# The first norm's factor moved behind its products, x turned unscaled, and the last columns ended in two pieces

## The chip, the cores and the metric

The kernel runs on one core of a Trainium2 chip. The metric is the device time of one execution in microseconds (us). Engines are named as the profile names them: PE (TensorE), DVE (VectorE), ACT (ScalarE), POOL (GpSimd), SP (SyncE, which here only issues DMAs).

## The reference

Two transformer blocks follow each other on x of 256 tokens and 1024 channels. The change touches the first norm with the product behind it, and the last norm:

```python
def _rms_norm(x, g):
    y = xf * lax.rsqrt(jnp.mean(xf * xf, axis=-1, keepdims=True) + EPS)
    return y * g
...
h = _rms_norm(x, g_pre_mix[l])
proj = h @ w_in[l]
qa, ka, va, c_q, c_kv, k_r, gate_logits = _split_cols(proj, [512, 512, 512, 384, 256, 32, 2048])
...
gates = sigmoid(gate_logits + b_gate[l])
...
return rms_norm(x, final_norm_g)
```

Rope then turns qa, ka and k_r by the positions; c_q and c_kv go through norms of their own into further products; two causal attentions of 8 heads use them; gates weigh their outputs. A second block with another attention and a routed table of 16384 experts follows, and its last product with the table `expert_v` ends in the last norm.

## The kernel before

Tokens lie on the 128 partitions in two halves, `tb` 0 and 1. Each product in float32 precision is made of three products of halved numbers (`mm3`, line 173): every operand is held as a rounded part (`hh`, `wh`) and a rest (`hl`, `wl`). A weight piece arrives by a DMA of SP into `raw`, ACT rounds it into `wh` (line 124), and DVE or POOL subtracts for `wl` (line 130). The pieces take turns: of three, two rests go to DVE and one to POOL.

The first norm (`norm_parts`, line 237, called at line 457) works on a half of x in this order: ACT squares x in two pieces with a sum (line 215), DVE makes the factor 1/sqrt in ten small instructions (`rsqrt`, lines 199 to 208), DVE multiplies x by factor and gain into `ny` (line 243), PE turns `ny` in eight 128x128 squares into two PSUM tiles `tps` (line 154), ACT copies each as `hh` (line 182) and DVE subtracts for `hl` (line 183). The gain row `g_pre_mix` is a DMA that ACT issues and that writes 512 KB, one copy of the row for each partition. The second half's turn is deferred (`defer`, `tick`) until the first half's products with the first weight block are issued.

`project` (line 273) then makes the columns of `w_in` block by block: 384 columns (c_q), 288 (c_kv and k_r), and three times 512 (qa, ka, va); each block has 24 products for each half of the tokens. What is done with a result stands in `emit_cq`, `emit_ckv`, `emit_rot` and `emit_va` (lines 480 to 496): ACT copies the sum from PSUM into `cnat`, and rope or a norm follows. The angles of rope are made by DVE (lines 538 to 547) and ACT (lines 548 to 550, with a load of ACT's table ahead) from the constants `cst` and the positions `post`. The columns of the gates come turned the other way, tokens along the free dimension (`stations`, line 314), in eight units between the heads of the attentions; `gate_done` lets ACT apply tanh to each.

At the end `v_units` adds up the products with `expert_v` in four PSUM tiles `po[tb][b]` of 512 columns. The last two units are ordered so that the tokens of half 0 end first, then columns 0 to 511 of half 1, then columns 512 to 1023 of it. `finish` (line 1131) follows each: DVE adds the residual (line 1136), ACT squares (line 1137), POOL multiplies by the gain (line 1138); after a half's second piece DVE makes the factor, ACT scales 512 columns (line 1142) and DVE the other 512 (line 1144), and ACT and SP each issue a DMA of the output.

All instructions are recorded by a framework that simulates a timeline to set the order on each engine; PE's matmuls are held in the written order (`in_line`). On an engine instructions run in the order that was set. Each of the DMA issues of SP and ACT takes one of eight semaphores in turn and waits until the transfer eight issues earlier has landed.

Of the kernel before, what the change touches and what calls it, by code (L numbers as in the profile page):

```python
# [9 lines left out]
F32 = mybir.dt.float32  # L10
# [23 lines left out]
RBUFS = 4  # L34
GAP = 120

# [43 lines left out]
def block_kernel(ctx: ExitStack, tc: tile.TileContext, a, out, dbg=None):  # L80
# [61 lines left out]

    def matmul(p, x, y, start, stop):
        in_line(pe.matmul(p, x, y, start=start, stop=stop))  # L144

# [7 lines left out]
    def turn(out, src):  # L153
        in_line(pe.transpose(out, src, ident))  # L154
# [17 lines left out]

    def mm3(p, xh, xl, yh, yl, first, last):
        matmul(p, xh, yh, first, False)
        matmul(p, xh, yl, False, False)
        matmul(p, xl, yh, False, last)

# [16 lines left out]

    def rsqrt(s0, s1=0.0):

# [10 lines left out]
        vec.tensor_scalar(t, t, -10.0 / 3.0, t, op0=OP.add, op1=OP.mult)  # L207
        vec.tensor_scalar(z, t, 5.0, z, op0=OP.add, op1=OP.mult)
        return z

    def rstd(srcs, junk, n):
# [5 lines left out]
        return rsqrt(s[:, 0:1], s[:, 1:2] if len(srcs) > 1 else 0.0)  # L217

# [252 lines left out]

    def cnat(p):
        c = wk.tile([P, 512], F32, name="cnat", bufs=2)
        if p is not None:
            copied[0] = act.activation(c[:, :p.shape[1]], p, AF.Copy)
        return c

    def emit_cq(tb, p):
        c = cnat(p)
        norm_parts(wk, c[:, :384], 384, gq, cqh[:, tb], cql[:, tb], 2)  # L480

    def emit_ckv(tb, p):
        c = cnat(p)
        rope(krr[tb], c[:, 256:288].rearrange("p (h d) -> p h d", h=1), rcos[:, tb, 8:24], rsin[:, tb, 8:24], 1, 16, wk)
        norm_parts(wk, c[:, :256], 256, gkv, ckh[:, tb], ckl[:, tb], 2)

    def emit_rot(dst):
        def emit(tb, p):
            c = cnat(p)
            rope(c.rearrange("p (h d) -> p h d", h=8)[:, :, :16], p.rearrange("p (h d) -> p h d", h=8)[:, :, :16],  # L490
                 rcos[:, tb, 0:8], rsin[:, tb, 0:8], 8, 8, wk)
            heads_T(c, 4, P, dst[:, tb])
        return emit

    def emit_va(tb, p):
        act.activation(va[:, tb, :], p, AF.Copy)

# [24 lines left out]
    pool.dma_start(out=tok, in_=a["consts"][:, C_I50:])  # L522
    i50, i128 = tok[:, :NCAND], tok[:, NCAND:]
# [109 lines left out]
    dump("x1", x)  # L633
    gpo = gain_row(xp, "g_post_mlp", D)
    g_n1 = gain_row(xp, "norm1_g", D)
# [77 lines left out]
    skey = const.tile([P, 2, P], F32, name="skey")  # L713
    pool.dma_start(out=skey, in_=a["sub_keys"])
    lng = gain_row(wk, "ln_v_g", 512, tag="lng")
# [390 lines left out]
    def v_units(us, done=None):  # L1106
# [23 lines left out]

    def finish(tb, b):
        c = slice(b * 512, (b + 1) * 512)
        if b == 0:
            fin[tb] = small.tile([P, 2], F32, name="ssq")
        s = fin[tb]
        vec.tensor_tensor(y[:, tb, c], y[:, tb, c], po[tb][b], op=OP.add)
        act.activation(z[:, 0, c], y[:, tb, c], AF.Square, scale=float(D) ** -0.5, accum_out=s[:, b:b + 1])  # L1137
# [42 lines left out]
def layout(i):  # L1180
# [49 lines left out]
```

## Time and profile before

| | us |
|---|---|
| median of 3 runs (lowest, highest) | 1324.47 (1322.88, 1325.99) |
| the profiled execution | 1322.9 |
| its span | 1321.1 |
| PE busy in it | 1287.6 (97%) |
| DVE, ACT, POOL busy | 932.0 (71%), 682.7 (52%), 405.4 (31%) |

A row of the timeline gives start, duration, engine, source line, operation, the tiles written and read, shapes, and in brackets how long the engine had been idle and what ended that. Rows of PE alone hold the products; weight loads (PEld) run beside them.

### The profile page before, as it was taken

What the parts mean: (1) busy time and instruction counts of PE and PEld (TensorE: products, weight loads), DVE (VectorE), ACT (ScalarE), POOL (GpSimd) and SP (SyncE); (2) the same over time, 40 slices, a digit from 0 to 9 for tenths busy, and PEclk for the clock granted to TensorE, in tenths of its full rate; (3) what the DMA queues carried; (4) which work ended last, traced back from release to release, by engine and by line L of the source; (5) the groups of instructions that cost most, each with busy time, mean ns of one, the idle gap of its engine ahead of it and who ended that gap; (6) DMA issues with size and microseconds to landing.
All of it is one profiled execution on the core that took longest, in us unless ns stands there. A gap on an engine that the chain in (4) does not pass through costs nothing.

```text
span 1321.1 us, 22724 instructions
## 1 busy us (share of the span) xinstructions
PE 1287.6 (97%) x8580; PEld 1144.6 (87%) x8580; DVE 932.0 (71%) x1924; ACT 682.7 (52%) x1046; POOL 405.4 (31%) x295
## 2 busy tenths in 40 slices
PE   6999999999998999999999999999999999999997
PEld 5788987899976777999999999999988888888885
DVE  6666777333357795799799699999955555555555
ACT  5576647455544655455564444444444444444443
POOL 3321335222244335300010499999700000000001
PEclk9999999999999999999999999999999999999999
DMA  8554565666645325456766544444476666666662
GB/s 287 169 174 129 183 201 168 215 192 191 191 139 188 113 80 178 126 155 181 226 188 197 172 145 146 147 142 149 154 231 195 194 192 193 194 195 195 194 192 81
DMA packets 64191, 230.65 MB, mean 175 GB/s; under 512 B 7280, under 2 KB 7696, under 8 KB 63952
## 3 DMA queue, kind: packets, MB, share of 16 engines
q1 hardware_dynamic: 61632, 221.03, 54.2%
q0 software_dynamic: 1728, 6.07, 1.3%
q10 hardware_dynamic: 720, 2.10, 0.4%
q8 instruction: 67, 1.10, 0.3%
q14 instruction: 44, 0.36, 0.1%
HBM read 227.07 MB, written 2.10 MB: 173 GB/s over the span
## 4 chain that ended last, share of the span: by engine, by line
PE 89%; DVE 5%; issue 3%; ACT 1%; DMA 1%; POOL 1%; SPq 0%; POOLq 0%; ACTq 0%; DVEq 0%
PE acc L144 52%; PE mid L144 35%; PE tps L154 2%; DVE wl L130 1%; DMA x<-in_x_dram 1%; POOL wl L130 1%; PE tps L144 1%; DVE cnat L339 0%; DVE rope_t L337 0%; DVE at_s L366 0%; ACT wh L124 0%; DVE ny L243 0%; DVE hl L183 0%; DVE rope_t L338 0%; DVE at_s L358 0%
## 5 line engine op out<-in xcount | busy, mean ns | idle before, releaser
L124 ACT ACTIVATE wh<-raw 128x1024 fp32r<-128x1024 f32 (+2 forms) x422 | 440.0, 1049 | 363.1 <-PE mid L144 161.8
L130 DVE TENSOR_TENSOR wl<-raw,wh 128x1024 fp32r<-128x1024 f32 (+1 forms) x350 | 443.7, 1269 | 216.4 <-ACT wh L124 214.0
L144 PE MATMUL mid<-hh,wh 128*128 128x256 f32 x1280 | 365.7, 286 | 0.0
L144 PE MATMUL mid<-hh,wl 128*128 128x256 f32 x1280 | 355.7, 278 | 0.0
L144 PE MATMUL mid<-hl,wh 128*128 128x256 f32 x1280 | 354.3, 277 | 0.0
L130 POOL TENSOR_TENSOR wl<-raw,wh 128x1024 fp32r<-128x1024 f32 (+3 forms) x72 | 177.5, 2475 | 323.9 <-ACT wh L124 273.0
L1080 POOL TENSOR_SCALAR m<-tok,key 128x128 bf16<-128x128 f32 x192 | 206.2, 1092 | 201.7 <-ACT key L953 120.4
L144 PEld LDWEIGHTS mid<-hl,wh 128*128 128x128 f32 x1280 | 241.2, 188 | 0.4
L144 PEld LDWEIGHTS mid<-hh,wh 128*128 128x128 f32 x1280 | 240.9, 188 | 0.4
L144 PEld LDWEIGHTS mid<-hh,wl 128*128 128x128 f32 x1280 | 240.4, 188 | 0.2
L144 PE MATMUL acc<-wl,ah 128*128 128x512 f32 x512 | 199.2, 389 | 0.0
L144 PE MATMUL acc<-wh,ah 128*128 128x512 f32 x512 | 199.2, 389 | 0.0
L144 PE MATMUL acc<-wh,al 128*128 128x512 f32 x512 | 199.2, 389 | 0.0
L144 PE MATMUL acc<-wh,hh 128*128 128x512 f32 (+2 forms) x288 | 115.8, 402 | 2.9 <-ACT hh L182 2.6
L144 PEld LDWEIGHTS acc<-wh,ah 128*128 128x128 f32 x512 | 96.1, 188 | 20.0
L144 PE MATMUL acc<-wl,hh 128*128 128x512 f32 (+2 forms) x288 | 112.2, 390 | 1.3 <-DVE wl L130 0.7
L144 PEld LDWEIGHTS acc<-wh,al 128*128 128x128 f32 x512 | 96.1, 188 | 20.0
L144 PEld LDWEIGHTS acc<-wl,ah 128*128 128x128 f32 x512 | 96.1, 188 | 19.8
L144 PE MATMUL acc<-wh,hl 128*128 128x512 f32 (+2 forms) x288 | 112.4, 390 | 0.8 <-DVE hl L183 0.6
L1138 POOL TENSOR_TENSOR hh<-hh,hl 128x512 f32<-128x512 f32 x4 | 5.1, 1284 | 344.9 <-ACT hl L1137 344.9
L182 ACT ACTIVATE ah<-acts 128x512 fp32r<-128x512 f32 x64 | 40.3, 632 | 88.8 <-PE acc L144 88.8
L183 DVE TENSOR_TENSOR al<-acts,ah 128x512 fp32r<-128x512 f32 x64 | 44.3, 693 | 52.0 <-ACT ah L182 52.0
(267 smaller groups left out, 1750.9 us busy)
## 6 DMA issues: line engine op xcount, KB each, us to landing
raw<-in_expert_u_dram SPq DMA_DIRECT2D x128, 512.0 KB, 3.8
raw<-in_expert_v_dram SPq DMA_DIRECT2D x128, 512.0 KB, 4.4
raw<-in_w_down_dram SPq DMA_DIRECT2D x32, 512.0 KB, 4.4
raw<-in_w_up_dram SPq DMA_DIRECT2D x24, 512.0 KB, 4.7
raw<-in_w_in_dram SPq DMA_DIRECT2D x20, 512.0 KB, 4.5
raw<-in_w_gate_dram SPq DMA_DIRECT2D x16, 512.0 KB, 4.6
raw<-in_w_out_dram SPq DMA_DIRECT2D x16, 512.0 KB, 4.4
raw<-in_w_in_n_dram SPq DMA_DIRECT2D x12, 512.0 KB, 4.5
```

Source lines behind the costliest of these rows:

```text
L124: i = act.activation(h[:, :n], raw[:, :n], AF.Copy)
L130: last_split[0] = eng.tensor_tensor(l[:, :n], raw[:, :n], h[:, :n].bitcast(F32), op=OP.subtract)
L144: in_line(pe.matmul(p, x, y, start=start, stop=stop))
L154: in_line(pe.transpose(out, src, ident))
L182: turned_[0] = act.activation(h, p, AF.Copy)
L183: vec.tensor_tensor(l, p, h.bitcast(F32), op=OP.subtract)
L1080: pool.tensor_scalar(m2, i128, key2[:, t:t + 1], None, op0=OP.is_equal)
L1138: pool.tensor_tensor(y[:, tb, c], y[:, tb, c], gfin[:, c], op=OP.mult)
```

## The change

The factor of the first norm no longer multiplies x. x is turned as it is, the gain multiplies the turned squares in PSUM (there it is one number per partition, so its DMA has 4 KB), and the products run on unscaled numbers. The factor `rx` of each half, made beside, then scales the results: ACT's copies take it as their scale, the rope tables are multiplied by it (`scs`), and for the gates, where tokens lie along the free dimension, a row of factors on all partitions (`rrow`) is made by two products with a diagonal and multiplied into PSUM by DVE ahead of each tanh. The second half of x is turned after the first 15 products. DMAs move from POOL to SP (`gq`, `gkv`, `tok`, `g_post_mlp`, `skey`), the identity from SP to ACT, and all four pieces of the first weight block are asked for ahead of the second half of x. At the end, columns 512 to 1023 of half 1 become two pieces of 256, and ACT scales 384 columns, DVE 640.

```diff
-GAP = 120
+GAP = 112
...
-    def transpose_split(src, nk, dsth, dstl):
+    def transpose_split(src, nk, dsth, dstl, gain=None):
...
                 turn(p[:, k, :], src[:, (k0 + k) * P:(k0 + k + 1) * P])
+            if gain is not None:
+                vec.tensor_tensor(p[:, :n, :], p[:, :n, :], gain[:, k0:k0 + n].unsqueeze(2).to_broadcast([P, n, P]), op=OP.mult)
             split(p[:, :n, :], dsth[:, k0:k0 + n, :], dstl[:, k0:k0 + n, :])
...
-    g_pre = gain_row(xp, "g_pre_mix", D, queue=act)
     ident = const.tile([P, P], F32, name="ident")
-    nc.sync.dma_start(out=ident, in_=a["ident"])
+    act.dma_start(out=ident, in_=a["ident"])
+    g_pre = const.tile([P, KB], F32, name="g_pre")
+    act.dma_start(out=g_pre, in_=a["g_pre_mix"])
     first = f"w_in_n{W1_BLOCKS[0][0]}"
-    for c0 in (0, 768):
-        loaded[first, 0, c0] = load(first, 0, c0, 768)
+    for n in range(2):
+        for c0 in (0, 768):
+            loaded[first, n, c0] = load(first, n, c0, 768)
     nc.sync.dma_start(out=x[1], in_=a["x"][1])
...
+    rx = []
+    transpose_split(x[0], KB, hh[:, 0], hl[:, 0], g_pre)
     for tb in range(TB):
-        norm_parts(wk, x[tb], D, g_pre, hh[:, tb], hl[:, tb], 1 + tb)
-    tick()
-    gq = gain_row(wk, "g_q_norm", 384, tag="gq")
-    gkv = gain_row(wk, "g_kv_norm", 256, tag="gkv")
+        junk = xp.tile([P, D], F32, name="ny", bufs=2)
+        rx.append(rstd([x[tb][:, :512], x[tb][:, 512:]], junk, D, wk.tile([P, 1], F32, name=f"rx{tb}")))
+    gq = gain_row(wk, "g_q_norm", 384, tag="gq", queue=nc.sync)
+    gkv = gain_row(wk, "g_kv_norm", 256, tag="gkv", queue=nc.sync)
...
-    def cnat(p):
+    def cnat(p, r=1.0):
...
-            copied[0] = act.activation(c[:, :p.shape[1]], p, AF.Copy)
+            copied[0] = act.activation(c[:, :p.shape[1]], p, AF.Copy, scale=r)
...
-                 rcos[:, tb, 0:8], rsin[:, tb, 0:8], 8, 8, wk)
+                 scs[:, tb, 0, :], scs[:, tb, 1, :], 8, 8, wk)
...
-    project(hh, hl, KB, [(f"w_in_n{W1_BLOCKS[0][0]}", 0, [(768, 768)] * 2, 384, emit_cq)])
+    for n, _ in enumerate(projecting(hh, hl, KB, [(f"w_in_n{W1_BLOCKS[0][0]}", 0, [(768, 768)] * 2, 384, emit_cq)])):
+        if n == 4:
+            transpose_split(x[1], KB, hh[:, 1], hl[:, 1], g_pre)
...
+    for tb in range(TB):
+        vec.tensor_scalar(scs[:, tb, 0, :], rcos[:, tb, 0:8], rx[tb], None, op0=OP.mult)
+        vec.tensor_scalar(scs[:, tb, 1, :], rsin[:, tb, 0:8], rx[tb], None, op0=OP.mult)
+        vec.tensor_scalar(diag[:, tb, :], ident, rx[tb], None, op0=OP.mult)
+
+    def factors_row():
+        p = tps([P, TB, P])
+        for tb in range(TB):
+            matmul(p[:, tb, :], ones, diag[:, tb, :], True, True)
+        act.activation(rrow, p.rearrange("p b t -> p (b t)"), AF.Copy)
+
+    defer(2, factors_row)
...
     def gate_done(u, p):
+        vec.tensor_tensor(p, p, rrow.unsqueeze(1).to_broadcast([P, 2, S]), op=OP.mult)
...
-        for blocks in ([[(0, 0), (0, 1)], [(1, 0)], [(1, 1)]] if last else [[(tb, b) for tb in range(TB) for b in range(2)]]):
+        for blocks in ([[(0, 0, 512), (0, 512, 512)], [(1, 0, 512)], [(1, 512, 256)], [(1, 768, 256)]] if last else
+                       [[(tb, c0, 512) for tb in range(TB) for c0 in (0, 512)]]):
...
+        if c0 + w < D:
+            if len(s) > 1:
+                vec.tensor_tensor(s[1], s[0], s[1], op=OP.add)
             return
...
-        act.activation(y[:, tb, :512], y[:, tb, :512], AF.Copy, scale=r)
-        act.dma_start(out=out[tb * P:(tb + 1) * P, :512], in_=y[:, tb, :512])
-        vec.tensor_scalar(y[:, tb, 512:], y[:, tb, 512:], r, None, op0=OP.mult)
-        nc.sync.dma_start(out=out[tb * P:(tb + 1) * P, 512:], in_=y[:, tb, 512:])
+        act.activation(y[:, tb, :384], y[:, tb, :384], AF.Copy, scale=r)
+        act.dma_start(out=out[t, :384], in_=y[:, tb, :384])
+        vec.tensor_scalar(y[:, tb, 384:], y[:, tb, 384:], r, None, op0=OP.mult)
+        nc.sync.dma_start(out=out[t, 384:], in_=y[:, tb, 384:])
```

What this makes of the order is seen at three places. The first is DVE at the start of the program; `rs_` names are the factor's ten steps, `ny` the scaled x, `tps` the turned squares in PSUM. Before:

```order
L536 MEMSET hpi 128x1
L199 TENSOR_SCALAR rs_x<-ssq 128x1
L200 TENSOR_SCALAR rs_y<-rs_x 128x1
...
L208 TENSOR_SCALAR rs_z<-rs_t,rs_z 128x1
L243 SCALAR_TENSOR_TENSOR ny<-x_87,rs_z,gain 128x512 x2
L130 TENSOR_TENSOR wl<-raw,wh 128x768
L183 TENSOR_TENSOR hl<-tps,hh 128x512
```

and now:

```order
L541 CAST posf<-post 128x2
L200 TENSOR_SCALAR rs_x<-ssq 128x1
L238 TENSOR_TENSOR tps<-tps,g_pre 128x512
L562 TENSOR_SCALAR bgate<-bgate 128x16
L201 TENSOR_SCALAR rs_y<-rs_x 128x1
L205 TENSOR_SCALAR rs_x_133<-rs_x 128x1
L238 TENSOR_TENSOR tps<-tps,g_pre 128x512
L130 TENSOR_TENSOR wl<-raw,wh 128x768
L202 TENSOR_SCALAR rs_t<-rs_y,rs_x 128x1
L184 TENSOR_TENSOR hl<-tps,hh 128x512 x2
```

The gain's product on the turned squares stands where the scaling of x stood, with the factor's steps strewn behind it; the cast of the positions, the first step of the factor and the gates' bias now stand ahead of it or between.

The second is PE at the first weight block, where three products of 384 columns make a step; `x_87` and `x_88` are the two halves of x:

```order
-L154 MATMUL tps<-ident,ny 128x128 x8
...
+L154 MATMUL tps<-ident,x_87 128x128 x8
 L144 MATMUL acc<-wh,hh 128x384
...
 L144 MATMUL acc<-wh,hl 128x384
+L154 MATMUL tps<-ident,x_88 128x128 x8
 L144 MATMUL acc<-wh,hh 128x384
...
 L144 MATMUL acc<-wh,hl 128x384
-L154 MATMUL tps<-ident,ny 128x128 x8
```

Turns and products are as many as before; the second half's eight turns stand after the first five steps of half 0 and not behind all eight.

The third is DVE at the end, from the factor of half 0 (`rs_z`) to the last sum. Before:

```order
L207 TENSOR_SCALAR rs_t<-rs_t 128x1
L208 TENSOR_SCALAR rs_z<-rs_t,rs_z 128x1
L1144 TENSOR_SCALAR hh<-hh,rs_z 128x512
L1136 TENSOR_TENSOR hh<-hh,acc 128x512
L199 TENSOR_SCALAR rs_x<-ssq 128x1
```

and now:

```order
L1166 TENSOR_TENSOR hh<-hh,acc 128x256
L210 TENSOR_SCALAR rs_z<-rs_t,rs_z 128x1
L1177 TENSOR_SCALAR hh<-hh,rs_z 128x640
L1171 TENSOR_TENSOR fin_14653<-fin_14637,fin_14653 128x1
L1166 TENSOR_TENSOR hh<-hh,acc 128x256
L200 TENSOR_SCALAR rs_x<-fin_14653,fin_14670 128x1
```

The last residual sum (`hh<-hh,acc`) has half the columns, and ahead of it stand the wider scaling of half 0 and a small sum of two square sums.

## Rows read from the trace of the kernel before

**Rows 1.** The page: engine, busy us (share of the span) and instructions.

```profile
PE 1287.6 (97%) x8580; PEld 1144.6 (87%) x8580; DVE 932.0 (71%) x1924; ACT 682.7 (52%) x1046; POOL 405.4 (31%) x295
```

**Rows 2.** PE's waits, first 240 us: total, times, longest us.

```profile
PE tps L154 <- DVE ny L243: 11.0, 2, 10.2
```

**Rows 3.** Timeline, half 0 of x up to its first products.

```profile
5.99 0.63 ACT L215 ACTIVATE ny<-x 128x512 f32<-128x512 f32 x1 [3.54 <-DMA x<-in_x_dram]
...
7.36 0.21 DVE L199 TENSOR_SCALAR rs_x<-ssq 128x1 f32<-128x1 f32 x1 [6.49 <-ACT ny L215]
...
8.60 0.84 ACT L124 ACTIVATE wh<-raw 128x768 fp32r<-128x768 f32 x1 [1.28 <-DMA raw<-in_w_in_n_dram]
...
9.41 1.41 DVE L243 SCALAR_TENSOR_TENSOR ny<-x,rs_z,gain 128x512 f32<-128x512 f32 x2
...
10.21 1.97 PE L154 MATMUL tps<-ident,ny 128*128 128x128 f32 x8 [10.21 <-DVE ny L243]
...
11.37 0.60 ACT L182 ACTIVATE hh<-tps 128x512 fp32r<-128x512 f32 x1
...
12.00 0.69 DVE L183 TENSOR_TENSOR hl<-tps,hh 128x512 fp32r<-128x512 f32 x1 [0.30 <-ACT hh L182]
```

**Rows 4.** Timeline, half 1 of x up to its first products.

```profile
13.09 0.63 ACT L215 ACTIVATE ny<-x 128x512 f32<-128x512 f32 x1 [1.13 <-DMA x<-in_x_dram]
...
13.23 0.52 PE L144 MATMUL acc<-wh,hh 128*128 128x384 f32 x1
...
16.87 0.95 DVE L130 TENSOR_TENSOR wl<-raw,wh 128x768 fp32r<-128x768 f32 x1
...
17.51 0.34 PE L144 MATMUL acc<-wl,hh 128*128 128x384 f32 x1
...
20.46 1.26 ACT L182 ACTIVATE hh<-tps 128x512 fp32r<-128x512 f32 x2 [0.23 <-PE tps L154]
...
21.84 0.44 PE L144 MATMUL acc<-wh,hl 128*128 128x384 f32 x1
```

**Rows 5.** Timeline, block of 288 columns and first block of 512.

```profile
28.65 0.40 PE L144 MATMUL acc<-wl,hh 128*128 128x288 f32 x1
...
33.83 2.80 POOL L130 TENSOR_TENSOR wl<-raw,wh 128x1024 fp32r<-128x1024 f32 x1 [5.24 <-ACT wh L124]
...
34.42 2.25 DVE L337 TENSOR_TENSOR rope_t<-cnat,rcos 128x16 f32<-128x16 f32 x1
...
37.17 1.21 DVE L130 TENSOR_TENSOR wl<-raw,wh 128x1024 fp32r<-128x1024 f32 x1
```

**Rows 6.** DMA issues of the first 30 us: KB each, median us to landing.

```profile
gain<-in_g_pre_mix_dram ACTq DMA_DIRECT2D x1, 512.0 KB, 5.4
...
post<-in_positions_dram POOLq DMA_DIRECT2D x1, 1.0 KB, 7.1
```

**Rows 7.** Two stretches: busy PE, PEld, DVE, ACT, POOL; granted clock, DMA share, GB/s.

```profile
12.00:14.00 2.00, 2.00 (x7) 1.76 (x7) 0.69 (x1) 0.91 (x3) 1.37 (x1) 1.00 1.04 416
...
80.00:155.00 75.00, 75.00 (x581) 66.97 (x580) 51.93 (x163) 54.60 (x132) 18.55 (x7) 1.00 0.44 142
```

**Rows 8.** Timeline, the end.

```profile
1311.13 1.29 POOL L1138 TENSOR_TENSOR hh<-hh,hl 128x512 f32<-128x512 f32 x1 [0.91 <-ACT hl L1137]
...
1311.27 1.43 DVE L1144 TENSOR_SCALAR hh<-hh,rs_z 128x512 f32<-128x512 f32 x1
...
1312.62 0.68 DVE L1136 TENSOR_TENSOR hh<-hh,acc 128x512 f32<-128x512 f32 x1
...
1313.33 0.63 ACT L1137 ACTIVATE hl<-hh 128x512 f32<-128x512 f32 x1 [1.35 <-DVE hh L1136]
...
1316.19 0.72 ACT L1142 ACTIVATE hh<-hh,rs_z 128x512 f32<-128x512 f32 x1 [2.14 <-DVE rs_z L208]
1316.21 0.49 DVE L1144 TENSOR_SCALAR hh<-hh,rs_z 128x512 f32<-128x512 f32 x1
```

**Rows 9.** One stretch of the second block, columns as in rows 7.

```profile
420.00:424.00 4.00, 3.91 (x13) 3.23 (x14) 4.00 (x8) 0.60 (x1) 0.00 (x0) 0.57 0.88 274
```

More of the change, by code (lines that the diff above doesn't have):

```diff
@@ L141, in block_kernel, with matmul @@
     late = []
-    def matmul(p, x, y, start, stop):
-        in_line(pe.matmul(p, x, y, start=start, stop=stop))
+    def matmul(p, x, y, start, stop, shared=False):
+        in_line(pe.matmul(p, x, y, start=start, stop=stop, skip_group_check=shared))
     def in_line(i):
@@ L171, in settle, with mm3 @@
             tick(100)
[L173 to L176, printed above, removed]
+    def mm3(p, xh, xl, yh, yl, first, last, shared=False):
+        matmul(p, xh, yh, first, False, shared)
+        matmul(p, xh, yl, False, False, shared)
+        matmul(p, xl, yh, False, last, shared)
     turned_ = [None]
@@ L192, in tps, with rsqrt @@
         return ps.tile(shape, F32, name="tps", bufs=2)
-    def rsqrt(s0, s1=0.0):
+    def rsqrt(s0, s1=0.0, out=None):
         x, x2, y, t, z = (small.tile([P, 1], F32, name=f"rs_{n}") for n in ("x", "x2", "y", "t", "z"))
@@ L207, in rsqrt, with rstd @@
         vec.tensor_scalar(t, t, -10.0 / 3.0, t, op0=OP.add, op1=OP.mult)
-        vec.tensor_scalar(z, t, 5.0, z, op0=OP.add, op1=OP.mult)
-        return z
-    def rstd(srcs, junk, n):
+        out = z if out is None else out
+        vec.tensor_scalar(out, t, 5.0, z, op0=OP.add, op1=OP.mult)
+        return out
+    def rstd(srcs, junk, n, out=None):
         s = small.tile([P, 2], F32, name="ssq")
@@ L216, in rstd @@
                                         accum_out=s[:, i:i + 1])
-        return rsqrt(s[:, 0:1], s[:, 1:2] if len(srcs) > 1 else 0.0)
+        return rsqrt(s[:, 0:1], s[:, 1:2] if len(srcs) > 1 else 0.0, out)
     def parts(pl=hp):
@@ L470, in block_kernel @@
     copied = [None]
-    def cnat(p):
+    def cnat(p, r=1.0):
         c = wk.tile([P, 512], F32, name="cnat", bufs=2)
         if p is not None:
-            copied[0] = act.activation(c[:, :p.shape[1]], p, AF.Copy)
+            copied[0] = act.activation(c[:, :p.shape[1]], p, AF.Copy, scale=r)
         return c
     def emit_cq(tb, p):
-        c = cnat(p)
+        c = cnat(p, rx[tb])
         norm_parts(wk, c[:, :384], 384, gq, cqh[:, tb], cql[:, tb], 2)
     def emit_ckv(tb, p):
-        c = cnat(p)
+        c = cnat(p, rx[tb])
         rope(krr[tb], c[:, 256:288].rearrange("p (h d) -> p h d", h=1), rcos[:, tb, 8:24], rsin[:, tb, 8:24], 1, 16, wk)
@@ L488, in emit @@
         def emit(tb, p):
-            c = cnat(p)
+            c = cnat(p, rx[tb])
             rope(c.rearrange("p (h d) -> p h d", h=8)[:, :, :16], p.rearrange("p (h d) -> p h d", h=8)[:, :, :16],
-                 rcos[:, tb, 0:8], rsin[:, tb, 0:8], 8, 8, wk)
+                 scs[:, tb, 0, :], scs[:, tb, 1, :], 8, 8, wk)
             heads_T(c, 4, P, dst[:, tb])
@@ L495, in emit_va @@
     def emit_va(tb, p):
-        act.activation(va[:, tb, :], p, AF.Copy)
+        act.activation(va[:, tb, :], p, AF.Copy, scale=rx[tb])
     def emit_uq(b):
@@ L521, in block_kernel @@
     tok = const.tile([P, C_N - C_I50], F32, name="tok")
-    pool.dma_start(out=tok, in_=a["consts"][:, C_I50:])
+    nc.sync.dma_start(out=tok, in_=a["consts"][:, C_I50:])
     i50, i128 = tok[:, :NCAND], tok[:, NCAND:]
@@ L551, in block_kernel @@
     vec.tensor_scalar(bgate, bgate, 0.5, None, op0=OP.mult)
+    scs = wk.tile([P, TB, 2, 8], F32, name="scs")
+    ones = wk.tile([P, P], F32, name="ones")
+    vec.memset(ones, 1.0)
+    diag = wk.tile([P, TB, P], F32, name="diag")
+    rrow = wk.tile([P, S], F32, name="rrow")
+    for tb in range(TB):
[8 more added lines that the diff above has]
+    defer(2, factors_row)
     project(hh, hl, KB, [(f"w_in_n{W1_BLOCKS[1][0]}", 0, [(576, 576)] * 2, 288, emit_ckv)])
@@ L633, in block_kernel @@
     dump("x1", x)
-    gpo = gain_row(xp, "g_post_mlp", D)
+    gpo = gain_row(xp, "g_post_mlp", D, queue=nc.sync)
     g_n1 = gain_row(xp, "norm1_g", D)
@@ L713, in block_kernel @@
     skey = const.tile([P, 2, P], F32, name="skey")
-    pool.dma_start(out=skey, in_=a["sub_keys"])
+    nc.sync.dma_start(out=skey, in_=a["sub_keys"])
     lng = gain_row(wk, "ln_v_g", 512, tag="lng")
@@ L1113, in v_units @@
         last = len(us) > 1
-        for blocks in ([[(0, 0), (0, 1)], [(1, 0)], [(1, 1)]] if last else [[(tb, b) for tb in range(TB) for b in range(2)]]):
+        for blocks in ([[(0, 0, 512), (0, 512, 512)], [(1, 0, 512)], [(1, 512, 256)], [(1, 768, 256)]] if last else
+                       [[(tb, c0, 512) for tb in range(TB) for c0 in (0, 512)]]):
             for u in us:
                 for n in range(2):
-                    for tb, b in blocks:
+                    for tb, c0, w in blocks:
                         t = slice(tb * P, (tb + 1) * P)
-                        c = slice(b * 512, (b + 1) * 512)
-                        mm3(po[tb][b], wt[u][0][:, n, t], wt[u][1][:, n, t], ws[u][n][0][:, c], ws[u][n][1][:, c],
-                            u + n == 0, u == NU - 1 and n == 1)
+                        c = slice(c0, c0 + w)
+                        mm3(po[tb][c0 // 512][:, c0 % 512:c0 % 512 + w], wt[u][0][:, n, t], wt[u][1][:, n, t], ws[u][n][0][:, c], ws[u][n][1][:, c],
+                            u + n == 0, u == NU - 1 and n == 1, c0 % 512 > 0)
             if last:
@@ L1129, in block_kernel, with finish @@
     fin = {}
[L1131 to L1137, printed above, removed]
+    def finish(tb, c0, w):
+        c = slice(c0, c0 + w)
+        s = fin.setdefault(tb, [])
+        s.append(small.tile([P, 1], F32, name=f"fin{len(s)}"))
+        vec.tensor_tensor(y[:, tb, c], y[:, tb, c], po[tb][c0 // 512][:, c0 % 512:c0 % 512 + w], op=OP.add)
+        act.activation(z[:, 0, c], y[:, tb, c], AF.Square, scale=float(D) ** -0.5, accum_out=s[-1])
         pool.tensor_tensor(y[:, tb, c], y[:, tb, c], gfin[:, c], op=OP.mult)
-        if b == 0:
+        if c0 + w < D:
+            if len(s) > 1:
+                vec.tensor_tensor(s[1], s[0], s[1], op=OP.add)
             return
-        r = rsqrt(s[:, 0:1], s[:, 1:2])
-        act.activation(y[:, tb, :512], y[:, tb, :512], AF.Copy, scale=r)
-        act.dma_start(out=out[tb * P:(tb + 1) * P, :512], in_=y[:, tb, :512])
-        vec.tensor_scalar(y[:, tb, 512:], y[:, tb, 512:], r, None, op0=OP.mult)
-        nc.sync.dma_start(out=out[tb * P:(tb + 1) * P, 512:], in_=y[:, tb, 512:])
+        r = rsqrt(s[-2], s[-1])
+        t = slice(tb * P, (tb + 1) * P)
+        act.activation(y[:, tb, :384], y[:, tb, :384], AF.Copy, scale=r)
+        act.dma_start(out=out[t, :384], in_=y[:, tb, :384])
+        vec.tensor_scalar(y[:, tb, 384:], y[:, tb, 384:], r, None, op0=OP.mult)
+        nc.sync.dma_start(out=out[t, 384:], in_=y[:, tb, 384:])
     pool.dma_start(out=y, in_=xres)
@@ L1188, in layout @@
     a["w_spatial"] = np.ascontiguousarray(i["w_spatial_2"][0].transpose(2, 0, 1))
-    for n in ("g_pre_mix", "g_q_norm", "g_kv_norm", "g_post_mix", "g_pre_mlp", "g_post_mlp"):
+    a["g_pre_mix"] = np.ascontiguousarray(i["g_pre_mix"].reshape(KB, P).T)
+    for n in ("g_q_norm", "g_kv_norm", "g_post_mix", "g_pre_mlp", "g_post_mlp"):
         a[n] = i[n].reshape(1, -1)
```

## The prediction

> **What bounds the kernel.** I read the page first: PE is busy for 1287.6 of the 1321.1 us of the span [rows 1]. So an edit pays only where PE stands still or where nothing but the end is left. PE's waits over the first 240 us come next: one kind stands out, the turns waiting for the scaled x (`ny`), 11.0 us in two waits, the longest 10.2 us, from the program's start [rows 2]. The timeline shows what fills it: x[0] lands and ACT squares it at 5.99, the first step of the factor is at 7.36, the scaling at 9.41, the turns at 10.21, the first `hh` at 11.37 and the first `hl` from 12.00 to 12.69 [rows 3]. The second half repeats it: squares at 13.09, `hh` at 20.46, and the first product that needs `hl` at 21.84 [rows 4]. Then PE waits for rests of weights: a product at 28.65, released by POOL, and the last rest of the first block of 512 columns, ending at 38.38 [rows 5]. Behind that PE runs on with few gaps; in the stretch of the gates it is busy for all of 75.00 us [rows 7]. What is saved ahead of 38.4 should therefore reach the end almost whole. The end itself is a chain of single steps [rows 8].
>
> **The start, step by step.**
>
> *x[0] lands sooner.* ACT's copy of the gain row, 512 KB, landed 5.4 us after its issue, beside x[0] [rows 6]. With the queues full the core moves 416 GB/s [rows 7], so without these 0.52 MB x[0] should land 1.26 us earlier, at 4.7 instead of just ahead of 5.99. Bounds: 4.4 (its first packets also faster) and 5.99 (no gain). I take 4.7.
>
> *Half 0.* Turns need x and the identity alone: 4.75 to 6.7 (1.97). The gain's product in PSUM is a DVE operation of 128x512 with one PSUM operand, as `hl` is: 0.69. It stands behind the first step of the factor, which needs the squares: 4.7 + 1.4 = 6.1, plus 0.21. So the product runs 6.3 to 7.0 and `hh` (0.60) ends at 7.6, where it ended at 11.97. DVE then has the second product (0.69), the first weight rest (0.95) and five small steps ahead of `hl`: it ends at about 9.4, where it ended at 12.69 [rows 3, 4]. The lead is 3.3 us.
>
> *Half 1.* DVE is now in a row: second `hl` 0.69, two weight rests at 0.95, which gives 12.0; then 13 small steps of some 0.2 us each less overlap, 14.0. x[1] has long landed. PE's turns of it stand behind 15 products, which run at half clock (0.52 us at 13.23 against 0.34 at 17.51 [rows 4]: 1.2 and 2.4 GHz) and end near 14.6. So the product with the gain is at 14.7 to 15.4, the second to 16.2, and `hl` ends at 17.2, where it ended at about 21.8. The lead is 4.6 us, and 22 equal products follow in both.
>
> *What is given back.* The sine and cosine with their table load, and the conversions of the 288 block, were ready behind half 1 before; now they come due at once. The clip of the angles meets POOL's rest of the first 576 piece and DVE's small steps wait for it, then sine, cosine, two conversions and the copy of half 1's result precede ACT's fourth piece. I get 25.0 for the end of POOL's fourth rest against 28.6 [rows 5]: a lead of 3.6 us. From there to 38.38 the order is the old one; the copy of `rrow` and the two added products (each no dearer than a turn, 1.97/8 = 0.25) cost at most 0.5 and partly lie in PE's remaining waits: I take 0.3. **Start: -3.3 us.** Bounds: -4.9 (4.6 kept and an early landing) and -1.0 (first rival).
>
> The eight `ny` scalings avoided on DVE equal the products with the gain (1.41 for two against 2 x 0.69), so DVE is not relieved; the gain comes from order alone. The moved DMAs (five fewer descriptor jobs on POOL, four more issues on SP) cost nothing: POOL's first rest waits for ACT, and SP's next pieces wait for buffers that come free by the weights' rests, which are earlier. If that cover were gone, late pieces would hold ACT at 288.
>
> **The gates.** Eight products of 128x512 in PSUM, 0.69 each as `hl` [rows 3]: 5.5 us more on DVE in 75 us in which it was busy 51.93 and PE never stopped [rows 7]. Tanh and the release of `acc` come 0.7 us later per unit. Ends: 0 and 5.5 if each were waited for; nearest to this case is that very stretch, where DVE work never stopped PE, so I take +0.2.
>
> **The end.** The last residual sum had been late already: DVE's scaling of half 0 took 1.43 us against 0.49 alone, ending with POOL's product over it (1311.13 + 1.29 = 1312.42), and the sum began at 1312.62 [rows 8]. Now the scaling has 640 columns, ends near 1312.8, a small sum follows, and the last residual sum begins about 1312.9: 0.3 lost. It has half the columns (by estimate 0.41 for 0.68), and so has the square (0.41 for 0.63): 0.5 won. The final scalings become 0.57 on ACT and 0.6 on DVE, where the longer was 0.72: 0.15 won, and the two output DMAs move as much as before. **End: -0.4**, between -0.8 and +0.5 (POOL's next product gets in first, about 0.65 to 0.9 later).
>
> A rule speaks against this part. The Trainium skill (GPSIMD Engine Reference, Specifications) says that POOL shares its SBUF interfaces with DVE, with contention for DVE instructions in a two-port mode or with two SBUF inputs. The trace agrees: the rope step of 16 columns took 2.25 us and ended with POOL's rest (33.83 + 2.80 = 36.63) [rows 5]. By that rule the scaling of 640 could be caught by two of POOL's products in turn, and the end would give +0.5 and the whole -2.6 instead of -3.5.
>
> **Sum.** -3.3 + 0.2 - 0.4 = -3.5 us. The profiled execution took 1322.9 (span 1321.1, 1.8 around it), 1.6 below the median of 1324.47; it would become 1319.4, and the median **1321.0 us**.
>
> **Rivals.**
>
> *DVE stands at the cast of the positions* (chance 0.30, with all other ways to lose most of the lead). The cast is now ahead of the first step of the factor and so of the first product with the gain. The positions took 7.1 us from issue to landing on POOL's queue [rows 6]; issued first there, a little after 1 us, and as slow, they would land at some 8.4, and everything behind moves by 2.3 us: start -1.0, total -1.2, 1323.3 us. For it: queue order is strict. Against: ahead of and around that DMA lay 512 KB and more, now gone from that queue. A late rise of PE's clock works alike: half 0 must then end at 0.3 us a product, and by 16 instead of 14 us some 0.5 us is lost.
>
> The Trainium skill (TensorE: Matmul & The Clock Gate, Part 1) says of the clock that "the default state is throttled, and activity releases the throttle". By that, turns at 4.7 with pauses behind them need not release it, as no row here can show. That would put the start at the lower figure just worked out.
>
> *More than forecast* (0.14). All of the 4.6 is kept, or a stretch vanishes that has no part in the edit: at 420 to 424 the granted clock was 0.57 on the mean [rows 9], a loss of 4 x 0.43 = 1.7 us, after a wait of PE. A shifted program may or may not meet it. Total -5.2: 1319.3 us.
>
> *The gates become a wait* (0.06): slower. DVE stands at a unit's product, which waits for PE, and softmax steps and weight rests queue behind; POOL's rests then hold those with two SBUF inputs, as the rope step shows. At 0.69 for the product and 0.4 for what slips behind, eight units cost 8.8 us, net +5.1: 1329.6 us. It decides once DVE has no slack within a head; its 23 idle of 75 us speak against that.
>
> **Numbers.** Forecast 0.50, less 0.30, more 0.14, slower 0.06. About 0.2% (2.65 us) can be told from no change: faster below 1321.8, slower above 1327.1. The forecast and "more" lie below 1321.8: 0.64 faster; the first rival gives 0.30 same; 0.06 slower. The range takes the forecast's bounds with the first rival and part of "more": 1318.4 to 1324.4, leaving out what is slower and the best cases.
>
> **What would show it.** Right: turns at 4.5 to 5, first `hh` ended by 8, the first `hl` product of half 1 near 17, POOL's fourth 576 rest ended near 25, the last 1024 rest of the next block near 35; no PE gap from 80 to 155; the last residual sum at some 0.3 us later against PE's last product. Wrong: DVE idle ahead of the cast or of the gates' bias for over 1 us; PE waits at the gates; x[0] landing at 6; the lead at 38.4 under 2 us.

## The result, and the profile after

The changed kernel takes 1333.77 us (median of 4 runs, 1333.0 to 1334.79), the kernel before 1325.23 in the 4 runs beside them: a ratio of 1.0064 [1.005, 1.0078], slower by 8.5 us, where the forecast was 3.5 us faster. The profiled execution took 1333.0 us, 10.1 more than the one of before.

The page of the kernel after has these busy times, which answer to [rows 1]:

```profile
span 1331.2 us, 22771 instructions
PE 1304.1 (98%) x8596; PEld 1158.1 (87%) x8596; DVE 936.3 (70%) x1941; ACT 684.1 (51%) x1049; POOL 397.4 (30%) x291
```

PE is busy for 16.5 us more than the 1287.6 of before. So the loss is no wait: PE takes longer over its work. The start, which the change is about, went nearly as forecast up to half 1's first products. Its timeline, answering to [rows 3, 4]:

```profile
4.63 0.63 ACT L217 ACTIVATE ny<-x 128x512 f32<-128x512 f32 x1 [1.69 <-DMA x<-in_x_dram]
4.87 1.97 PE L154 MATMUL tps<-ident,x 128*128 128x128 f32 x8 [4.87 <-DMA ident<-in_ident_dram]
6.10 0.17 DVE L541 CAST posf<-post 128x2 f32<-128x2 int32 x1 [5.07 <-DMA post<-in_positions_dram]
...
6.30 0.69 DVE L238 TENSOR_TENSOR tps<-tps,g_pre 128x512 f32<-128x512 f32 x1
7.02 0.60 ACT L183 ACTIVATE hh<-tps 128x512 fp32r<-128x512 f32 x1 [0.32 <-DVE tps L238]
...
9.93 0.69 PE L144 MATMUL acc<-wh,hl 128*128 128x384 f32 x1
...
17.78 0.44 PE L144 MATMUL acc<-wh,hl 128*128 128x384 f32 x1 [0.21 <-DVE hl L184]
```

x[0] is squared at 4.63 instead of 5.99, the turns follow at 4.87, the first `hh` ends at 7.62, and half 1's first product that needs `hl` comes at 17.78 instead of 21.84. To see where the lead goes I set the starts of ACT's weight conversions (422 in either kernel) of both traces against each other. After minus before: -2.7 us at 8.6 us, -1.75 at 41.7, +1.25 at 257, +2.3 at 410, -0.7 at 430, +2.4 at 640, +6.2 at 740, +10.5 at 972, and +10.5 still at 1302. A lead is lost steadily, and most of it in the second block's stations, where nothing was edited. Two stretches of that part, first of the kernel before (length, then busy time and count of PE, PEld, DVE, ACT and POOL, granted clock, DMA share, GB/s):

```profile
660.00:720.00 60.00, 60.00 (x532) 60.00 (x531) 58.73 (x122) 32.65 (x42) 5.29 (x6) 1.00 0.62 190
1000.00:1060.00 60.00, 60.00 (x266) 49.69 (x265) 34.59 (x33) 29.23 (x34) 0.00 (x0) 1.00 0.64 193
```

and of the kernel after, with the stretch of the gates from [rows 7] on top:

```profile
80.00:155.00 75.00, 74.28 (x568) 66.07 (x566) 54.34 (x168) 54.33 (x130) 17.41 (x7) 1.00 0.41 134
660.00:720.00 60.00, 60.00 (x512) 60.00 (x511) 55.89 (x120) 31.56 (x40) 5.01 (x6) 1.00 0.63 186
1000.00:1060.00 60.00, 60.00 (x266) 49.69 (x265) 34.59 (x33) 29.23 (x34) 0.00 (x0) 1.00 0.64 193
```

PE never pauses from 660 to 720 in either, its clock is granted in full in both (2.4 GHz), and yet it gets through 512 products instead of 532: 0.117 us each instead of 0.113. From 1000 on, in the products with `expert_v`, both do 266. The slow ones are the products of the stations: 256 columns of `hh` or `hl` move past a square of weights from the ring, the pool of weight buffers that the products use in turn. The starts of single products show it, first in the kernel before, then in experiment e2 below, which has the ring where the kernel after has it:

```profile
679.80 0.28 PE L144 MATMUL mid<-hh,wl 128*128 128x256 f32 x1
679.91 0.28 PE L144 MATMUL mid<-hh,wh 128*128 128x256 f32 x1
680.02 0.28 PE L144 MATMUL mid<-hl,wh 128*128 128x256 f32 x1
680.14 0.28 PE L144 MATMUL mid<-hh,wl 128*128 128x256 f32 x1
```

```profile
679.72 0.28 PE L144 MATMUL mid<-hh,wh 128*128 128x256 f32 x1
679.84 0.28 PE L144 MATMUL mid<-hl,wh 128*128 128x256 f32 x1
679.96 0.28 PE L144 MATMUL mid<-hh,wl 128*128 128x256 f32 x1
680.08 0.28 PE L144 MATMUL mid<-hh,wh 128*128 128x256 f32 x1
```

### The profile page after: what moved, and what is told of

Read it like the earlier page. It is cut to its first block, busy times and chain, and to the rows that moved or that the text cites. A ratio compares the mean times of both kernels' runs of the same rounds, so it can differ in the third digit from the quotient of the medians.

```text
span 1331.2 us, 22771 instructions
## 1 busy us (share of the span) xinstructions
PE 1304.1 (98%) x8596; PEld 1158.1 (87%) x8596; DVE 936.3 (70%) x1941; ACT 684.1 (51%) x1049; POOL 397.4 (30%) x291
## 4 chain that ended last, share of the span: by engine, by line
PE 85%; DVE 4%; ACT 1%; issue 1%; DMA 0%; ACTq 0%; DVEq 0%
PE acc L144 48%; PE mid L144 35%; PE tps L154 1%; DVE wl L130 1%; PE tps L144 1%; DMA raw<-in_w_branch_dram 0%; DVE at_s L370 0%; DVE cnat L343 0%; ACT ny L257 0%; ACT wh L124 0%; DVE hl L184 0%; DVE at_s L362 0%; DVE rope_t L342 0%; DVE cnat L432 0%; DVE rope_t L341 0%
## 5 line engine op out<-in xcount | busy, mean ns | idle before, releaser
L1110 POOL TENSOR_SCALAR m<-tok,key 128x128 bf16<-128x128 f32 x192 | 201.2, 1064 | 217.6 <-ACT key L983 124.5
L144 PE MATMUL acc<-wh,ah 128*128 128x512 f32 (+1 forms) x516 | 200.0, 388 | 0.5 <-DVE hh L1166 0.5
L144 PE MATMUL acc<-wh,al 128*128 128x512 f32 (+1 forms) x516 | 199.9, 387 | 0.0
L144 PE MATMUL acc<-wl,ah 128*128 128x512 f32 (+1 forms) x516 | 199.9, 387 | 0.0
L1168 POOL TENSOR_TENSOR hh<-hh,hl 128x512 f32<-128x512 f32 (+1 forms) x5 | 5.5, 1112 | 344.2 <-ACT hl L1167 344.2
```

The costliest lines, as they stand in the source:

```text
L144: in_line(pe.matmul(p, x, y, start=start, stop=stop, skip_group_check=shared))
L1110: pool.tensor_scalar(m2, i128, key2[:, t:t + 1], None, op0=OP.is_equal)
```

## The experiments

**The theory.** What these products have in common is not an instruction but a place. The diff cuts `GAP` from 120 to 112 floats, 32 bytes, which makes up for the new constant `g_pre`. It makes up for nothing else. The new `finish` takes its sums from three new names, `fin0`, `fin1` and `fin2`, in the pool `small`, which has four buffers for each name, and a buffer of one float takes 32 bytes: 3 x 4 x 32 = 384 bytes ahead of the ring. In the compiled kernels `raw` begins at byte 13312 of a partition before and at 13696 after, one `wh` buffer at 62464 and at 62848; `hh` and `hl`, filled from the right end, stay (one `hh` at 145344). Rivals: the gates' added work on DVE, or the new start or end, slow PE.

**e1: the whole change, the ring put back.**

```diff
-GAP = 112
+GAP = 16
```

> The whole change, with the gap ahead of the ring of weight buffers cut from 112 to 16 floats, so that the ring lies at the SBUF addresses of the kernel before (raw at byte 13312 of a partition, wh at 62464) and not 384 bytes further. Theory (place of the ring): the products of the stations cost 0.1128 us each again in the stretch of 60 us that I compare, the lag of 10 us does not build up, and the time is 1320 to 1322 us, below the kernel before. Rival (the gates' added work on DVE, or the start, holds PE): the place is nothing, the pitch stays 0.117 us, and the time stays at 1333 us, as the changed kernel.

Measured: 1321.76 us (11 runs), ratio to before 0.9978 [0.9967, 0.9989], which makes it 2.9 us faster than the kernel before, whose runs beside it had a median of 1325.92 (e1 to e4 share them). The medians alone lie 4.2 us apart; the gains given below are by the ratios. The stretch has its pace again:

```profile
660.00:720.00 60.00, 60.00 (x532) 60.00 (x531) 58.94 (x124) 32.43 (x40) 5.29 (x6) 1.00 0.61 189
```

With the place alone undone, 12.0 us come back by the medians (1333.77 to 1321.76), 11.4 by the two ratios to before.

**e2: the kernel before, only the ring moved.**

```diff
-GAP = 120
+GAP = 216
```

> The kernel before with nothing but the gap enlarged from 120 to 216 floats, so that the ring moves by the 384 bytes of the changed kernel. Theory (place of the ring): 0.117 us per product of the stations and 1335 to 1339 us, 10 to 14 us slower. Rival (the loss comes from the gates or the start): 1325 us, no change.

Measured: 1334.09 us (5 runs), ratio 1.007 [1.0056, 1.0084]. An unused tile 384 bytes larger costs as much as the whole change did:

```profile
660.00:720.00 60.00, 60.00 (x512) 60.00 (x511) 55.09 (x120) 31.25 (x39) 5.01 (x6) 1.00 0.60 184
```

By its median it is 8 us slower and by its ratio 9, a little less than expected; by profiled executions 11.4 (1334.26 to 1322.9).

**e3 and e4: the two parts of the change, each alone with the ring in its old place.** e3 takes back the part at the end:

```diff
-        s = fin.setdefault(tb, [])
-        s.append(small.tile([P, 1], F32, name=f"fin{len(s)}"))
+        if b == 0:
+            fin[tb] = small.tile([P, 2], F32, name="ssq")
+        s = fin[tb]
```

(with `blocks`, `mm3`'s call and the 512-column scalings of before). e4 is the kernel before with the new `blocks`, `finish` and 384/640 scalings, and

```diff
-GAP = 120
+GAP = 24
```

> The change without its part at the end (the last columns in two pieces of 512 as before, so no fin tiles, and the ring at its old place). Theory (place of the ring): 1321.5 to 1323.5 us, a gain of 2 to 3.5 us, of which the start gives 2.3 to 3.3 and the gates take back up to 0.7. Rival (gates or start hold PE): 1333 us or a little more.

> The kernel before with the change's part at the end alone (256-wide pieces, 384 and 640 columns), and the gap cut from 120 to 24 floats, so that the fin tiles do not move the ring. Theory (place of the ring): the end gives 0.2 to 0.6 us, 1324.6 to 1325.0 us, and the time from the last product's last sum to the end of the span goes from 8.5 to about 7.4. Rival (the end itself is dear, by its order): 1333 us.

Measured: e3 1321.41 us (7 runs), ratio 0.9978 [0.9962, 0.9994]; e4 1324.0 us (11 runs), ratio 0.9994 [0.9983, 1.0006]. The start with the gates gives 2.9 us (0.8 to 5.0). The end is not dear, as its rival had it, but whether it gives anything is not decided: -0.8 us, between -2.3 and +0.8. The traces don't decide it either. From ACT's last weight conversion to the end of the span, against the kernel before, the changed end took 0.4 us less (after and e1) and 0.3 more (e4), the unchanged end 0.65 less (e3) and the same (e2).

**e7: the gates without the factor.** It leaves out the factor of the first norm in the gates:

```diff
     def gate_done(u, p):
-        vec.tensor_tensor(p, p, rrow.unsqueeze(1).to_broadcast([P, 2, S]), op=OP.mult)
```

> The whole change with the ring at its old place (gap of 16 floats), without the multiplication of the gates' products by the row of factors: the gates leave the factor of the first norm out. The difference to the same kernel with it (1321.8 us) is what the eight multiplications cost. Theory (place of the ring explains the loss, and DVE has room there): 0 to 0.7 us less, 1321.1 to 1321.8 us. Rival (the gates become a wait): 3 to 9 us less.

Measured: 1322.56 us (11 runs), ratio to the kernel before beside it (1325.26) 0.9979 [0.9969, 0.9988], where e1 had 0.9978. The eight multiplications cost nothing that can be measured, within the 1 to 2 us of these intervals. In the traces their lead over before dips within the stretch (with them from -1.9 at 81 to -0.9 at 119 and back to -1.5 at 156; without, -1.7, -1.6, -1.55).

**e5, e6, e8: is it the place of the weights by itself?** In the kernel before I saw two paces among the stations of one stretch (257 to 330 us), 0.1133 us and 0.118 to 0.120, going by buffer. The slowest buffers began at bytes that leave 448 when divided by 512 (448 modulo 512), as `hh` does; the ring stood at 0. My reading was that the weights want a multiple of 512. So the right side, and those two buffers with it, were moved to 0:

```diff
-    gapr.tile([P, 8], F32, name="gapr")
+    gapr.tile([P, 120], F32, name="gapr")
```

e6 has this edit together with e1's, e8 only another gap:

```diff
-GAP = 120
+GAP = 184
```

(In the text of e5 these two buffers are said to be of the pool `wkx`; they belong to `wk` of line 623, pool `wkm`, on the right.)

> The kernel before, with the pad at the right end of SBUF enlarged from 8 to 120 floats: the tiles that are filled from the right (hh and hl of every norm, and the two weight buffers of wkx, which the stations use in turn with the ring) move by 448 bytes, from 448 to 0 modulo 512; the ring stays. In the kernel before, products of the stations at 257 to 290 us alternate by buffer between starts 0.1133 us apart (ring, at 0 modulo 512) and 0.1178 us apart (wkx, at 448). Theory (the place of the operand that is loaded as PE's weights decides, modulo 512 bytes): the 0.1178 us vanish and the time falls by 4 to 9 us, to 1316 to 1321 us. Rival 1 (the distance between the two operands decides, or a place in one certain bank): the stations of the ring slow down instead, since hh moved against it: 1330 us or more. Rival 2 (wkx is slow for another reason): 1325 us.

> The whole change with the ring at its old place (gap of 16 floats) and the pad at the right enlarged to 120 floats. Theory (place modulo 512 bytes): the gains add: 4 to 9 us below the 1321.8 us of the change with only the ring put back, 1313 to 1318 us, which is below both kernels. Rival: no less than 1321 us.

> The kernel before with the gap of 184 floats: the ring lies 256 bytes further, at 256 modulo 512. If any place off a multiple of 512 bytes costs the same: starts 0.1177 us apart in the stretch 660 to 720, 1334 us. If a multiple of 256 bytes is enough, 0.1135 us and 1325 us. If the cost goes by how much of a row lies beyond a border, something between.

Measured: e5 1340.43 us (4 runs), ratio 1.012 [1.01, 1.0139]; e6 1340.79 (4 runs), ratio 1.0117 [1.0101, 1.0132], where 1313 to 1318 was expected; e8 1323.25 (one run, beside 1325.26). My reading fell: with weights and `hh` both at 0 the stations are slower than before or after, 0.120 us. Rival 1, the distance between the two, was right. e8 agrees: moved by 256 bytes, the ring keeps its pace. The stretch in e5, then in e8:

```profile
660.00:720.00 60.00, 60.00 (x503) 60.00 (x502) 52.59 (x118) 31.13 (x39) 4.91 (x6) 1.00 0.61 181
660.00:720.00 60.00, 60.00 (x532) 60.00 (x532) 59.00 (x123) 32.63 (x42) 5.30 (x6) 1.00 0.63 191
```

**e9: both sides moved, the distance kept.**

```diff
-GAP = 120
+GAP = 216
...
-    gapr.tile([P, 8], F32, name="gapr")
+    gapr.tile([P, 40], F32, name="gapr")
```

> The kernel before with the ring 384 bytes further, as in the changed kernel, and the tiles at the right 128 bytes back (pad of 40 floats instead of 8). Modulo 512 both have moved by the same 384 bytes, so that the distance between the stations' two operands is the old one and each place is new. If the distance decides: starts 0.1135 us apart at 660 to 720 and 1324 to 1326 us, against 1334 with the ring alone moved. If the places themselves decide (the ring at 0 or 256 modulo 512 is good, 384 bad): 0.117 us or more and 1333 us or more.

Measured: 1324.65 us (10 runs) beside 1324.39, ratio 0.9997 [0.9982, 1.0012]. The ring lies where it does in e2, at 384 modulo 512, and nothing is lost. Its starts:

```profile
679.73 0.28 PE L144 MATMUL mid<-hh,wh 128*128 128x256 f32 x1
679.85 0.28 PE L144 MATMUL mid<-hl,wh 128*128 128x256 f32 x1
679.96 0.28 PE L144 MATMUL mid<-hh,wl 128*128 128x256 f32 x1
680.07 0.28 PE L144 MATMUL mid<-hh,wh 128*128 128x256 f32 x1
```

**e10: every distance at once.** Weight buffers of 1032 floats instead of 1024:

```diff
-            h = pl.tile([P, 1024], F32R, name="wh", bufs=cycle.count(pl))
-            l = pl.tile([P, 1024], F32R, name="wl", bufs=cycle.count(pl))
+            h = pl.tile([P, 1032], F32R, name="wh", bufs=cycle.count(pl))
+            l = pl.tile([P, 1032], F32R, name="wl", bufs=cycle.count(pl))
```

> The kernel before with weight buffers of 1032 floats instead of 1024 (the last 8 unused), so that the sixteen wh and wl buffers of the ring start at sixteen different places modulo 512, 32 bytes apart, and hh stays at 448. One run then shows the distance between starts for each place of the weights. If the distance of the two operands modulo 256 decides: 0.1133 us at distances near 64 (weights at 0 and 256), 0.117 to 0.120 at 0 and at 192, and the same values 256 bytes further on; between them this run says. If places of 0 modulo 256 are good by themselves: only those at 0 and 256 fast. Time between 1325 and 1335 us.

Measured: 1344.75 us (one run), slower than I expected, since the products with `expert_v` slow down too, 260 in this stretch for the 266 of before:

```profile
1000.00:1060.00 60.00, 60.00 (x260) 48.50 (x260) 33.95 (x33) 28.62 (x33) 0.00 (x0) 1.00 0.61 186
```

For every pair of neighbouring 256-column products I took the time between their starts from the trace, and the places of the running product's `hh` or `hl` and of the next one's weights from the compiled kernel (modulo 512; distance is weights less `hh`):

```
kernel   hh   weights  distance  pairs  median ns  mean ns
before   448    0         64     3868     114       114.6
before   448  448          0       92     120       119.9
after    448  384        448     3873     118       117.7
e5         0    0          0     3965     120       119.5
e8       448  256        320     3868     114       114.6
e9       320  384         64     3868     114       114.7
e10      448    0         64      530     113       114.7
e10      448   32         96      520     119       118.6
e10      448   64        128      532     119       119.4
e10      448   96        160      520     118       119.0
e10      448  128        192      284     114       115.5
e10      448  160        224      285     119       119.1
e10      448  192        256      286     118       117.9
e10      448  224        288      285     120       121.0
```

Distances of 64 and 320 are good and 0 and 448 bad wherever they were tried alone. In e10 neighbours differ in place, so a row there is not a single distance; by it 192 is good too, and 128, 256 and the odd multiples of 32 are bad. The table leaves out e10's rarer places; among them some 15 pairs at distance 320 took 120 ns, where e8 has 114. What rule makes a distance good was not found. In every run but e10 the weights of neighbouring products stand alike modulo 512, so the table can't tell the weights of the running product from those of the next; that the next one's count is argued from their being loaded meanwhile.

**e11: the changed kernel, the other side moved to restore the distance.**

```diff
-    gapr.tile([P, 8], F32, name="gapr")
+    gapr.tile([P, 40], F32, name="gapr")
```

> The changed kernel, line for line, with the ring where it lies in it (384 bytes further), but the pad at the right end 40 floats instead of 8, so that hh and hl lie 128 bytes lower and the distance modulo 512 between the stations' operands is that of the kernel before. Theory (the distance decides, and the rest of the change gives what was forecast): starts 0.1135 us apart at 660 to 720 and 1320 to 1323 us, 12 us below the changed kernel and 2 to 4 below the kernel before. Rival (something else of the change costs too): above 1326 us.

Measured: 1321.53 us (12 runs, 1317.42 to 1326.78) beside 1322.69, ratio 0.9982 [0.9969, 0.9996]. That is 12.2 us below the changed kernel (10.9 by the two ratios), and 2.4 us below the kernel before, where e1 is 2.9 below (the medians beside each other are 1.2 apart). The time came as expected, the starts did not: the profiled execution, which was the slowest of the 12 runs, had the changed kernel's pace in this stretch, for a reason that the last section takes up.

```profile
660.00:720.00 60.00, 60.00 (x512) 60.00 (x511) 56.58 (x121) 31.74 (x40) 5.01 (x6) 1.00 0.60 187
```

## Why the prediction was wrong

**The step that failed** is "What is saved ahead of 38.4 should therefore reach the end almost whole". It took the 1280 us behind the start as the same work at the same pace. The sum has a term for each instruction that is added or moved, and none for the tiles: the `fin` buffers and the cut of `GAP` stood in the diff, and adding up the bytes ahead of the ring (-32 + 32 + 384) would have shown that it moves. What a move costs I had read in no row of before, though its trace has the two paces among the stations at 257 to 330 us. By the table, the 256-column products alone cost (117.7 - 114.6) ns x some 3870 = 12.0 us. No rival held this; the one for "slower" put the loss at the gates, which e7 clears.

**The rest of the sum stood in its total, less so in its parts.** With the distance restored the change gives 2.9 us (e1, 1.5 to 4.4) and 2.4 (e11, 0.5 to 4.1), where 3.5 were forecast. The start gave about half of its term, so that the near agreement is in part luck. In the traces of e1, e3 and e11 the lead grows by 0.35 to 0.7 us between 41.7 and 257 us, which the sum did not have (in e7 it falls by 0.4).

*The start* had -3.3, and the runs show -1.6 to -1.8 by 41.7 us (after, e1, e3, e7, e11). In the kernel after it held up to the end of POOL's rest of the fourth 576 piece: 23.80 + 1.42 = 25.22 against a forecast 25.0. (The `ny` scalings that it avoids are four, not eight; the sum does not hang on it.) Then "From there to 38.38 the order is the old one" failed, in the block of 512 columns, answering to [rows 5]:

```profile
23.80 1.42 POOL L130 TENSOR_TENSOR wl<-raw,wh 128x576 fp32r<-128x576 f32 x1 [2.81 <-ACT wh L124]
...
30.46 2.50 POOL L130 TENSOR_TENSOR wl<-raw,wh 128x1024 fp32r<-128x1024 f32 x1 [5.23 <-ACT wh L124]
...
30.75 3.30 DVE L130 TENSOR_TENSOR wl<-raw,wh 128x1024 fp32r<-128x1024 f32 x1
...
34.10 0.50 PE L144 MATMUL acc<-wl,hh 128*128 128x512 f32 x1 [1.67 <-DVE wl L130]
...
34.84 1.21 DVE L130 TENSOR_TENSOR wl<-raw,wh 128x1024 fp32r<-128x1024 f32 x1
```

In the earlier schedule POOL's rest caught DVE's small rope step. Now it catches a rest of weights that PE needs next: 3.30 us instead of 1.21, and PE waits 1.67, where it waited 0.3 in that stretch before. The last rest ends at 36.05, 2.3 us ahead of 38.38. This is the collision of POOL and DVE that I had priced for the end, and had left out here. e3, e7 and e11 have it too. In e1 (and e6) the lead was lost earlier and by something else: DVE stood at the first step of the angles, until the constants landed, and the product with the gain behind it came late.

```profile
15.40 0.38 DVE L549 TENSOR_SCALAR ang<-cst,posf 128x24 f32<-128x24 f32 x2 [1.62 <-DMA cst<-in_consts_dram]
...
18.42 0.44 PE L144 MATMUL acc<-wh,hl 128*128 128x384 f32 x1 [0.52 <-DVE hl L184]
...
25.35 1.43 POOL L130 TENSOR_TENSOR wl<-raw,wh 128x576 fp32r<-128x576 f32 x1 [3.75 <-ACT wh L124]
...
32.59 2.26 DVE L341 TENSOR_TENSOR rope_t<-cnat,rcos 128x16 f32<-128x16 f32 x1
```

There the rest of the fourth piece ended at 26.78, and POOL's next one caught the small rope step again; the lead at 41.7 us was 1.8 all the same.

*The first rival cost next to nothing where it was placed.* Its sign came: DVE idled 5.07 us ahead of the cast, until the positions landed. But they took 4.8 us from issue to landing and not 7.1, so that the cast stood at 6.10 and not at 8.4, and the factor's first step behind it needs ACT's squares, which ended at 5.97. The same kind of wait, for the constants, is the one that held e1 for 1.62 us, and the kernel after for 0.72.

*The gates* (+0.2): nothing measurable by time. In the kernel after PE idles 0.7 of 75 us there, where it idled not at all, and DVE has 2.4 us more; in e1 PE idles 0.1.

*The end* (-0.4): not decided, as e4 says. Its rows, answering to [rows 8], went partly as worked out:

```profile
1322.12 1.14 DVE L1177 TENSOR_SCALAR hh<-hh,rs_z 128x640 f32<-128x640 f32 x1
...
1323.18 0.68 DVE L1171 TENSOR_TENSOR fin<-fin,fin 128x1 f32<-128x1 f32 x1
...
1323.79 0.41 DVE L1166 TENSOR_TENSOR hh<-hh,acc 128x256 f32<-128x256 f32 x1
...
1324.23 0.42 ACT L1167 ACTIVATE hl<-hh 128x256 f32<-128x256 f32 x1 [1.22 <-DVE hh L1166]
...
1326.89 0.55 DVE L1177 TENSOR_SCALAR hh<-hh,rs_z 128x640 f32<-128x640 f32 x1
```

Sum and square of 256 columns take 0.41 and 0.42 and the last scaling of 640 takes 0.55, close to the estimates, and from the start of the last residual sum to the end it is 7.4 us (1323.79 to 1331.2) for 8.5 (1312.62 to 1321.1). But the small sum of squares takes 0.68 us under POOL's product, and PE has a wait that I missed:

```profile
1321.95 0.38 PE L144 MATMUL acc<-wh,ah 128*128 128x256 f32 x1 [0.51 <-DVE hh L1166]
```

The two pieces of 256 share a PSUM tile, so the second piece's products wait until DVE has read the first.

**How the profiled 10.1 us add up**, as far as they do: stations about +12.0; the 768 products of 512 columns with `hh` or `hl` as weights, 230.6 to 233.2 ns on the mean, +2.0; 384 more with `mfh` or `mfl` as weights, 230.2 to 232.2, +0.8; start -1.75; a stall near 420 us that the kernel after doesn't have -3.1 (the lag from 410 to 430); end -0.4. That is some +9.5; the other 0.6 was not assigned. The stall was the chance named under "More than forecast", priced there at 1.7 us for the clock alone; PE also idles 2.2 us less from 415 to 431 (busy 14.95 us instead of 12.78). [rows 9] had a granted clock of 0.57, and after has

```profile
420.00:424.00 4.00, 3.85 (x19) 3.24 (x20) 4.00 (x5) 1.07 (x2) 2.25 (x1) 1.00 0.62 215
```

So it is no gain of the edit: e1, the same change at the old pace, has the stall (clock 0.74), and e2, which has none of the change, lost it (1.00). Nor does the pace alone decide: e4 at the old pace had 1.00, and e5 and e6, the slowest in the stations, 0.72 and 0.77. What decides it stays open.

## What to carry to other kernels

Where PE is the bound, an edit's price includes the place of every tile behind the ones it adds: a few small buffers, here 384 bytes, cost about four times what the edit gave. Add up the bytes that a change puts ahead of long-lived operands, compare the address table of both kernels, and compare the time between starts in a stretch that was not edited. If PE's busy time grows and its count of products hardly does (8580 to 8596 here), look at operands' places before waits.

## What was not expected of the hardware

The pace of a 256-column product here hangs on the distance within SBUF between the operand that streams and the weights: 0.1133 us at best and 0.120 at worst, with PE's clock granted in full. The Trainium skill (TensorE: Matmul & The Clock Gate, Step-by-step: what each phase is for) says: "Loading the next tile's weights doesn't steal SBUF read bandwidth from the running matmul." The runs here do not fit with that as it stands: e2 and e9 differ only in where `hh`, `hl` and the other tiles on the right lie, and by 0.003 us a product on the mean. That both reads meet in one part of the memory would explain it, but was not shown. Nor is one distance best for all: the 512-column products with `hh` or `hl` as weights took 230.6 ns before, 233.2 after and 229.1 in e5, where the 256-column ones are slowest.

At a good distance there are two paces, 0.1133 and 0.1178, and the pace was seen to switch at a break in the stream. In e11's profiled execution, its slowest run, the stations ran at 0.1178 from about 624 us, until the turns at 729:

```profile
728.75 0.28 PE L144 MATMUL mid<-hh,wh 128*128 128x256 f32 x1
728.87 0.28 PE L144 MATMUL mid<-hl,wh 128*128 128x256 f32 x1
728.98 0.28 PE L144 MATMUL mid<-hh,wl 128*128 128x256 f32 x1
729.10 0.38 PE L154 MATMUL tps<-ident,f 128*128 128x128 f32 x2
...
729.79 0.28 PE L144 MATMUL mid<-hh,wh 128*128 128x256 f32 x1
729.90 0.28 PE L144 MATMUL mid<-hl,wh 128*128 128x256 f32 x1
730.01 0.28 PE L144 MATMUL mid<-hh,wl 128*128 128x256 f32 x1
```

At a bad distance nearly all products keep the slow pace (after: 97 of 3578 pairs of station products were fast, before: 2910 of 3569). That may be why the 12 runs of e11, at a good distance, spread over 9 us and the 4 of the kernel after over less than 2; the spread's cause was not tested.
